# A chunked RWKV-7 recurrence inside one fused block: 64-column products turned into whole-array products, and the output products gathered behind the loop

## The chip, the cores and the metric

The kernel runs on one core of one Trainium2 chip. The metric is the device time of one execution in microseconds (us). Below, PE is the tensor engine (matmuls), PEld its weight loads, DVE the vector engine, ACT the scalar engine, POOL the GpSimd engine, SP the engine that issues most DMAs.

## The reference, cut to what matters

One transformer block on 512 tokens of width 2048: an RWKV-7 time mix with 16 heads of 64, a sparse attention, gates, an output projection and an MLP. The change touches the time mix alone. For each head it scans over the tokens:

```python
def step(S, inp):
    r_t, w_t, k_t, v_t, kk_t, a_t = inp
    sa = jnp.einsum('bhij,bhj->bhi', S, -kk_t)
    S = S * w_t[:, :, None, :] + sa[..., None] * (kk_t * a_t)[:, :, None, :] + v_t[..., None] * k_t[:, :, None, :]
    return S, jnp.einsum('bhij,bhj->bhi', S, r_t)
```

S is a 64x64 state per head. All arrays are float32.

## The kernel before, in words

The scan is done in chunks of 64 tokens: eight chunks (`NCH`), and heads in pairs, so eight passes (`hp`, 0 to 7) over a pair of heads. `stage1` does for each pair: `gates` (the inputs of the scan), `inner` (all products inside a chunk, for all chunks at once) and `outer` (the recurrence from chunk to chunk). The change is in `outer`, L536 to L575.

The state M of both heads is one 128x128 tile: head 0 in rows and columns 0 to 63, head 1 in 64 to 127, zeros elsewhere (`self.Ms`, two tiles that take turns). For chunk c, `outer` issues in this order:

- L550, PE: WT of the chunk (128 rows, 64 columns) times M, into half of the partitions of the PSUM tile `pu` (tile name `seq`, one buffer). L551, DVE: VU of the chunk is U0 less that product.
- L552, PE: M times the queries AR of the chunk, added into 64 columns of the PSUM tile `py`, which collects the output of all chunks.
- L556, POOL: the decayed state Mf, for the next M.
- L557, a "pump": some steps of other work for PE (below).
- L562, PE: for each head the keys KBn (64 columns) times VU (64 columns), into 64 partitions of the PSUM tile `pm` (`seq` again). L566 and L568, DVE: the next M, one instruction a head.
- L572, PE: for each head VU (64 columns) times the scores S (64 columns), added into `py`.
- L575, another pump.

So M waits for `pm`, the next L550 for M, VU for L550, and `pm` for VU: a chain that goes back and forth between PE and DVE. A float32 matmul of the program stands in the trace as two records of PE and two weight loads; they are called passes below. A matmul whose output has 64 columns of weights works in a 128x64 part of the array (the trace writes 128*64), and the two heads of L562 and of L572 sit in the two halves.

The other work is a list of projection jobs (`add_job`): each step (`step`, L104 to L106) is three matmuls with 128x128 weights and 512 columns, in the split format that the kernel uses for its projections, and counts as three filler passes. `pump(t)` adds t times a rate to a credit and issues steps while the credit lasts; the rate of a pair of heads is set so that its jobs (`FILL`) last through it. What is left is issued by `drain()` at the end of the pair. PE and POOL run in the order written; the order of DVE, ACT and SP is chosen by the scheduler of the compiler. The weights of a step come by DMA (L66), are rounded by ACT (L67), and DVE forms the remainder (L68). After the loop come a pump (L579), ACT's square and copy of `py` (L581, L583), a pump, and the sums over a head (L599) for the norm.

Of the kernel before, what the change touches and what calls it, by code (L numbers as in the profile page):

```python
# [17 lines left out]
OP = mybir.AluOpType  # L18
# [5 lines left out]
C = 64  # L24
NCH = T // C
# [27 lines left out]
class Kern:  # L53
# [236 lines left out]
    def stage1(self):  # L290
        nc, tc, a = self.nc, self.tc, self.a
        with ExitStack() as ctx:
# [56 lines left out]
            for j in range(2):  # L349
                m = p.tile([128, 128], F32, name=f"M{j}")  # L350
                nc.gpsimd.memset(m, 0.0)
# [40 lines left out]
    def t2(self, name, bufs=1):  # L392
        return self.p1.tile([128, T], F32, name=name, bufs=bufs)
# [142 lines left out]
    def outer(self, hp, cur):  # L536

        nc, p, pp, t2, big = self.nc, self.p1, self.ps1, self.t2, self.big
        AR, KBn, VU, f, bv, g, S, U0, WT = (cur[n] for n in ("AR", "KBn", "VU", "f", "bv", "g", "S", "U0", "WT"))

        py = pp.tile([128, T], F32, name="py", bufs=1)
        M = None
        for c in range(NCH):
            q, cp = c % 2, c // 2
            us = slice(64 * q, 64 * q + 64)
            if M is None:
                nc.scalar.copy(VU[us, c], U0[us, cp])
            else:
                pu = pp.tile([128, T], F32, name="seq", bufs=1)
                nc.tensor.matmul(pu[us, 0:128], WT[:, cp, us], M, start=True, stop=True)  # L550
                nc.vector.scalar_tensor_tensor(VU[us, c], pu[us, 0:128], -1.0, U0[us, cp], op0=OP.mult, op1=OP.add)  # L551
                nc.tensor.matmul(py[:, C * c:C * c + C], M, AR[:, 1, C * c:C * c + C], start=False, stop=False)  # L552
            Mn = self.Ms[c % 2]
            if M is not None and c < NCH - 1:
                Mf = p.tile([128, 128], F32, name="Mf", bufs=1)
                nc.gpsimd.tensor_scalar(Mf, M, f[:, c:c + 1], None, op0=OP.mult)  # L556
            self.pump(PUMP["u"])  # L557
            if c < NCH - 1:
                pm = pp.tile([128, T], F32, name="seq", bufs=1)
                for h in range(2):  # L560
                    hs = slice(64 * h, 64 * h + 64)
                    nc.tensor.matmul(pm[hs, 0:64], KBn[:, c, hs], VU[:, c, hs], start=True, stop=True)  # L562
                for h in range(2):
                    hs = slice(64 * h, 64 * h + 64)
                    if M is None:
                        nc.vector.tensor_scalar(Mn[hs, hs], pm[hs, 0:64], f[hs, c:c + 1], None, op0=OP.mult)  # L566
                    else:
                        nc.vector.scalar_tensor_tensor(Mn[hs, hs], pm[hs, 0:64], f[hs, c:c + 1], Mf[hs, hs],  # L568
                                                       op0=OP.mult, op1=OP.add)
            for h in range(2):  # L570
                hs = slice(64 * h, 64 * h + 64)
                nc.tensor.matmul(py[hs, C * c:C * c + C], VU[:, c, hs], S[:, h, c, 64:128],  # L572
                                 start=c == 0, stop=c == NCH - 1)
            if c < NCH - 1:
                self.pump(PUMP["m"])  # L575
            M = Mn


        self.pump(PUMP["gn0"])  # L579
        sq = t2("sq")  # L580
        nc.scalar.activation(sq, py, AF.Square)  # L581
        y = t2("tha")
        nc.scalar.copy(y, py)  # L583
        self.pump(PUMP["gn2"])
        ye = self.head_rsqrt(self.head_sums(sq), 1.0 / 64, GN_EPS, None)
        self.pump(PUMP["gn3"])
        rs = self.head_bcast(ye)
        nc.vector.tensor_tensor(y, y, rs, OP.mult)
        nc.vector.scalar_tensor_tensor(y, y, self.par("lnx_w", hp), bv, op0=OP.mult, op1=OP.add)
        yo = t2("yo")  # L590
        nc.vector.scalar_tensor_tensor(yo, y, self.par("lnx_b", hp), g, op0=OP.add, op1=OP.mult)
        nc.sync.dma_start(self.yd[hp], yo)
# [957 lines left out]
```

## Time and profile before

| | |
|---|---|
| time, median of 3 runs | 3124.81 us (3119.63 to 3130.18) |
| time of the profiled execution | 3125.73 us |
| its span, first to last instruction | 3124.0 us |
| granted TensorE clock, mean of the span | 0.993 of full speed |
| PE busy | 3050.8 us, 98% of the span |
| PE weight loads busy | 2591.8 us, 83% |
| DVE, ACT, POOL busy | 59%, 38%, 19% |

The profiled execution is one run; its span leaves out 1.7 us before the first and after the last instruction. A pass of PE lasts longer than the distance to the next one, since passes are pipelined: what a pass costs is read from the starts of neighbours, not from its length. Stage 1's eight pairs of heads lie between about 95 and 950 us.

### The profile page before, as it was taken

The page shows a single profiled execution, that of the slowest core. Times are in us where ns is not written, and L with a number is a line of the kernel's source. Part 1 is how long each engine was busy: PE and PEld are TensorE (multiplying, and loading weights), DVE is VectorE, ACT ScalarE, POOL GpSimd, SP SyncE. Part 2 cuts the span into 40 slices and gives each one's busy share as a digit, 9 for nine tenths or more (in the row PEclk, how much of TensorE's full clock was granted, in tenths as well). Part 3 has the DMA queues.
Part 4 walks back from the last instruction along what each step waited for, and adds up shares of the span by engine and source line. Part 5 has one row for each costly group of instructions (what it writes and reads, how often), then busy time and mean ns, then how long its engine had stood idle before and what let it go on. Part 6 is the DMA issues. An engine that isn't in the chain of part 4 may idle for free.

```text
span 3124.0 us, 49657 instructions
## 1 busy us (share of the span) xinstructions
PE 3050.8 (98%) x19296; PEld 2591.8 (83%) x19296; DVE 1855.4 (59%) x3312; ACT 1192.9 (38%) x2031; POOL 588.6 (19%) x613
## 2 busy tenths in 40 slices
PE   9999999999999999999999899999999999999998
PEld 7777777777777877787888899999997888888998
DVE  7855756575563457775464877777775232344565
ACT  4322333233232335654333444444444232232454
POOL 2312222231231000001221533333330000000012
PEclk9999999999999999999999999999999999999999
DMA  4222222222224422225543344444446243253465
GB/s 163 82 85 75 82 78 74 71 82 83 77 79 142 135 95 65 65 78 189 169 144 128 133 135 128 131 135 134 128 130 204 94 139 103 94 165 118 148 193 176
DMA packets 165596, 369.28 MB, mean 118 GB/s; under 512 B 18672, under 2 KB 24304, under 8 KB 157168
## 3 DMA queue, kind: packets, MB, share of 16 engines
q1 hardware_dynamic: 154080, 339.28, 33.7%
q10 hardware_dynamic: 10640, 24.73, 2.1%
q8 instruction: 151, 2.47, 0.3%
q0 software_dynamic: 640, 2.10, 0.2%
q14 instruction: 85, 0.70, 0.1%
HBM read 322.06 MB, written 41.94 MB: 117 GB/s over the span
## 4 chain that ended last, share of the span: by engine, by line
PE 62%; DVE 2%; DMA 1%; POOL 1%; issue 0%; ACT 0%; SPq 0%; DVEq 0%; ACTq 0%; POOLq 0%
PE acc L1263 20%; PE acc L104 13%; PE acc L106 12%; PE acc L105 12%; PE po L1043 1%; PE sc L1010 1%; PE pt L1032 1%; DMA wraw<-w_down 1%; DVE wlo L68 0%; DMA u<-ud 0%; PE sc L954 0%; POOL rb L1177 0%; DMA raw<-w_up 0%; PE po L989 0%; POOL sq L1175 0%
## 5 line engine op out<-in xcount | busy, mean ns | idle before, releaser
L67 ACT CAST whi<-wraw 128x512 fp32r<-128x512 f32 x752 | 465.8, 620 | 1065.9 <-PE acc L105 989.2
L68 DVE TENSOR_TENSOR wlo<-wraw,whi 128x512 fp32r<-128x512 f32 x752 | 530.7, 707 | 567.6 <-ACT whi L67 560.0
L104 PE MATMUL acc<-xn,whi 128*128 128x512 f32 x1472 | 611.5, 415 | 1.3 <-DVE th L387 1.3
L106 PE MATMUL acc<-xn,wlo 128*128 128x512 f32 x1472 | 578.2, 393 | 0.0
L105 PE MATMUL acc<-xn,whi 128*128 128x512 f32 x1472 | 577.1, 392 | 0.0
L104 PE MATMUL acc<-xs,whi 128*128 128x512 f32 (+1 forms) x1280 | 449.5, 351 | 5.4 <-ACT xs L932 5.4
L105 PE MATMUL acc<-xs,whi 128*128 128x512 f32 (+1 forms) x1280 | 449.1, 351 | 2.0 <-DVE xs L933 2.0
L106 PE MATMUL acc<-xs,wlo 128*128 128x512 f32 (+1 forms) x1280 | 448.8, 351 | 0.1
L1263 PE MATMUL acc<-hx,hs 128*128 128x256 f32 x2048 | 369.8, 283 | 3.1 <-ACT hs L1248 3.1
L106 PEld LDWEIGHTS acc<-xn,wlo 128*128 128x128 f32 x1472 | 277.3, 188 | 61.6
L104 PEld LDWEIGHTS acc<-xn,whi 128*128 128x128 f32 x1472 | 278.1, 189 | 60.0 <-issue 6.5
L1263 PEld LDWEIGHTS acc<-hx,hs 128*128 128x128 f32 x2048 | 317.4, 190 | 3.3 <-ACT hs L1248 3.3
L105 PEld LDWEIGHTS acc<-xn,whi 128*128 128x128 f32 x1472 | 278.7, 189 | 46.0
L1263 PE MATMUL acc<-hx,ls 128*128 128x256 f32 x1024 | 289.2, 282 | 2.1 <-DVE ls L1249 2.1
L1263 PE MATMUL acc<-hx,h 128*128 128x256 f32 x1536 | 277.8, 283 | 5.0 <-ACT h L1240 5.0
L104 PEld LDWEIGHTS acc<-xs,whi 128*128 128x128 f32 x1280 | 241.4, 189 | 41.2 <-ACT xs L932 6.4
L105 PEld LDWEIGHTS acc<-xs,whi 128*128 128x128 f32 x1280 | 241.4, 189 | 38.4 <-DVE xs L933 3.5
L106 PEld LDWEIGHTS acc<-xs,wlo 128*128 128x128 f32 x1280 | 241.4, 189 | 35.5 <-DVE wlo L68 0.5
L1263 PEld LDWEIGHTS acc<-hx,h 128*128 128x128 f32 x1536 | 237.7, 190 | 5.4 <-ACT h L1240 5.4
L1249 DVE TENSOR_TENSOR ls<-s,hs 128x1024 fp32r<-128x1024 f32 x128 | 184.5, 1441 | 74.6 <-ACT hs L1248 74.5
L1263 PE MATMUL acc<-hx,l 128*128 128x256 f32 x768 | 216.5, 282 | 1.8 <-DVE l L1241 1.8
L1263 PEld LDWEIGHTS acc<-hx,ls 128*128 128x128 f32 x1024 | 195.8, 191 | 2.3 <-DVE ls L1249 2.3
(354 smaller groups left out, 4225.3 us busy)
## 6 DMA issues: line engine op xcount, KB each, us to landing
wraw<-w_down SPq DMA_DIRECT2D x320, 256.0 KB, 3.2
raw<-w_up SPq DMA_DIRECT2D x64, 1024.0 KB, 5.2
wraw<-w_gate SPq DMA_DIRECT2D x128, 256.0 KB, 3.0
wraw<-w_rkv SPq DMA_DIRECT2D x96, 256.0 KB, 3.1
wraw<-w_o SPq DMA_DIRECT2D x64, 256.0 KB, 3.1
ud<-f ACTq DMA_DIRECT2D x32, 512.0 KB, 6.2
u<-ud SPq DMA_DIRECT2D x32, 512.0 KB, 5.3
thd<-th SPq DMA_DIRECT2D x32, 256.0 KB, 3.5
```

Source lines behind the costliest of these rows:

```text
L67: nc.scalar.copy(hi, raw)
L68: lo_eng.tensor_tensor(lo, raw, hi.bitcast(F32), OP.subtract)
L104: nc.tensor.matmul(ps, hi[:, j], xh, start=opens and k == 0, stop=False)
L105: nc.tensor.matmul(ps, hi[:, j], xl, start=False, stop=False)
L106: nc.tensor.matmul(ps, lo[:, j], xh, start=False, stop=close and last)
L1010: nc.tensor.matmul(ps[:, 0:n], q, self.kst[h][:, x, br, 0:n], start=x == 0, stop=x == 1)
L1032: nc.tensor.transpose(pt[:, b], s[:, 128 * b:128 * b + 128], self.ident)
L1043: nc.tensor.matmul(self.o[j][64 * h:64 * h + 64, 128 * i:128 * i + 128], self.vn[:, b, v0:v0 + 64], pT[h][:, b], start=False, stop=i == 3 ...
L1249: nc.vector.tensor_tensor(l, s, h.bitcast(F32), OP.subtract)
L1263: nc.tensor.matmul(o, w[wi][part][:, 128 * i:128 * i + 128], x[:, xi, xp], start=kh == 0 and i == 0 and m == 0 and slot in opens, stop=kh ...
```

## The change

Three edits in `outer`. L550 takes both chunks of WT (128 columns of weights) and writes all 128 partitions of `pu`; the half that is read is the same. The two products of L562 become one with 128 columns of weights and 128 columns of VU; of its result the two diagonal blocks are read. L572's sixteen products leave the loop and are issued behind it, first the eight chunks of head 0, then the eight of head 1; `py` is opened by the product of L552 of chunk 1 in place of L572 of chunk 0. The pumps stay where they are.

```diff
-                nc.tensor.matmul(pu[us, 0:128], WT[:, cp, us], M, start=True, stop=True)
+                nc.tensor.matmul(pu[:, 0:128], WT[:, cp], M, start=True, stop=True)
                 nc.vector.scalar_tensor_tensor(VU[us, c], pu[us, 0:128], -1.0, U0[us, cp], op0=OP.mult, op1=OP.add)
-                nc.tensor.matmul(py[:, C * c:C * c + C], M, AR[:, 1, C * c:C * c + C], start=False, stop=False)
+                nc.tensor.matmul(py[:, C * c:C * c + C], M, AR[:, 1, C * c:C * c + C], start=c == 1, stop=False,
+                                 skip_group_check=True)
...
-                for h in range(2):
-                    hs = slice(64 * h, 64 * h + 64)
-                    nc.tensor.matmul(pm[hs, 0:64], KBn[:, c, hs], VU[:, c, hs], start=True, stop=True)
+
+                nc.tensor.matmul(pm[:, 0:128], KBn[:, c], VU[:, c], start=True, stop=True)
...
-                        nc.vector.tensor_scalar(Mn[hs, hs], pm[hs, 0:64], f[hs, c:c + 1], None, op0=OP.mult)
+                        nc.vector.tensor_scalar(Mn[hs, hs], pm[hs, hs], f[hs, c:c + 1], None, op0=OP.mult)
                     else:
-                        nc.vector.scalar_tensor_tensor(Mn[hs, hs], pm[hs, 0:64], f[hs, c:c + 1], Mf[hs, hs],
+                        nc.vector.scalar_tensor_tensor(Mn[hs, hs], pm[hs, hs], f[hs, c:c + 1], Mf[hs, hs],
                                                        op0=OP.mult, op1=OP.add)
-            for h in range(2):
-                hs = slice(64 * h, 64 * h + 64)
-                nc.tensor.matmul(py[hs, C * c:C * c + C], VU[:, c, hs], S[:, h, c, 64:128],
-                                 start=c == 0, stop=c == NCH - 1)
             if c < NCH - 1:
                 self.pump(PUMP["m"])
             M = Mn
+        for h in range(2):
+            hs = slice(64 * h, 64 * h + 64)
+            for c in range(NCH):
+                nc.tensor.matmul(py[hs, C * c:C * c + C], VU[:, c, hs], S[:, h, c, 64:128], start=False,
+                                 stop=c == NCH - 1, skip_group_check=True)
```

## Rows read from the trace of the kernel before

**Rows 1.** The profile's page: busy time by engine.

```profile
PE 3050.8 (98%) x19296; PEld 2591.8 (83%) x19296; DVE 1855.4 (59%) x3312; ACT 1192.9 (38%) x2031; POOL 588.6 (19%) x613
```

**Rows 2.** Windows: stage 1, and the loop of the first pair; columns in the second line.

```profile
core 0: us, PE busy (x) PEld busy (x) DVE busy (x) ACT busy (x) POOL busy (x), PEclk, DMA share, GB/s
160.00:950.00 790.00, 771.94 (x5129) 590.53 (x5128) 476.81 (x948) 239.74 (x449) 203.13 (x286) 1.00 0.24 79
162.58:190.84 28.26, 28.26 (x166) 19.22 (x165) 12.14 (x30) 5.60 (x9) 3.63 (x6) 1.00 0.22 75
```

**Rows 3.** Timeline of PE, one chunk (start, length to the last end, operation, count).

```profile
168.13 0.39 PE L105 MATMUL acc<-xn,whi 128*128 128x512 f32 x1
168.36 0.39 PE L106 MATMUL acc<-xn,wlo 128*128 128x512 f32 x1
168.68 0.43 PE L550 MATMUL seq<-M,WT 128*64 128x128 f32 x2
169.04 0.43 PE L552 MATMUL py<-AR,M 128*128 128x64 f32 x2
169.28 0.47 PE L104 MATMUL acc<-xn,whi 128*128 128x512 f32 x1
169.60 0.39 PE L105 MATMUL acc<-xn,whi 128*128 128x512 f32 x1
169.82 0.40 PE L106 MATMUL acc<-xn,wlo 128*128 128x512 f32 x1
170.15 0.34 PE L562 MATMUL seq<-VU,KBn 128*64 128x64 f32 x4
170.32 0.29 PE L572 MATMUL py<-S,VU 128*64 128x64 f32 x4
170.53 0.50 PE L104 MATMUL acc<-xn,whi 128*128 128x512 f32 x1
170.87 0.39 PE L105 MATMUL acc<-xn,whi 128*128 128x512 f32 x1
...
172.80 0.43 PE L550 MATMUL seq<-M,WT 128*64 128x128 f32 x2
```

**Rows 4.** Timeline of the weight loads around L741, then around L702, whole-array products.

```profile
265.36 1.09 PEld L741 LDWEIGHTS un<-Z,Q 128*128 128x128 f32 x8
...
260.79 0.97 PEld L702 LDWEIGHTS un<-Df,N 128*128 128x128 f32 x8
261.69 0.19 PEld L104 LDWEIGHTS acc<-xn,whi 128*128 128x128 f32 x1
```

**Rows 5.** Timeline of PE at the same two places.

```profile
265.35 0.39 PE L106 MATMUL acc<-xn,wlo 128*128 128x512 f32 x1
265.58 1.00 PE L741 MATMUL un<-Z,Q 128*128 128x64 f32 x8
...
262.03 0.39 PE L105 MATMUL acc<-xn,whi 128*128 128x512 f32 x1
```

**Rows 6.** Instructions of L550 and L572 (ns min/median/max).

```profile
L550 PE MATMUL seq<-M,WT x112: 272/298/324, 164.6 to 946.7; 128*64 128x128 f32 x112
...
L572 PE MATMUL py<-S,VU x256: 221/222/271, 162.7 to 948.8; 128*64 128x64 f32 x128
```

**Rows 7.** Timeline at the end of the first pair's loop.

```profile
190.52 0.40 PE L106 MATMUL acc<-xn,wlo 128*128 128x512 f32 x1
190.85 0.34 PE L572 MATMUL py<-S,VU 128*64 128x64 f32 x4
191.11 0.50 PE L104 MATMUL acc<-xn,whi 128*128 128x512 f32 x1
191.23 0.60 ACT L581 ACTIVATE sq<-py 128x512 f32<-128x512 f32 x1 [1.09 <-PE py L572]
```

**Rows 8.** Timeline of DVE in the chunk of rows 3.

```profile
168.85 0.69 DVE L68 TENSOR_TENSOR wlo<-wraw,whi 128x512 fp32r<-128x512 f32 x1 [1.79 <-ACT whi L67]
169.57 0.28 DVE L551 SCALAR_TENSOR_TENSOR VU<-seq,U 64x128 f32<-64x128 f32 x1
170.60 0.60 DVE L568 SCALAR_TENSOR_TENSOR M<-seq,f,Mf 64x64 f32<-64x64 f32 x2 [0.75 <-PE seq L562]
```

**Rows 9.** Timeline in the pair with the fewest fillers.

```profile
497.05 0.29 DVE L568 SCALAR_TENSOR_TENSOR M<-seq,f,Mf 64x64 f32<-64x64 f32 x1
497.56 0.19 PEld L550 LDWEIGHTS seq<-M,WT 128*64 128x64 f32 x2 [0.36 <-DVE M L568]
```

**Rows 10.** Waits of PE, 160 to 950 us (us in total, times, longest).

```profile
PE big L619 <- ACT sq L612: 12.1, 8, 3.9
...
PE seq L550 <- DVE M L568: 0.8, 1, 0.8
```

## The prediction

> **What bounds the kernel now.** I read the page first, then windows of the stage that changes, then the timeline of one chunk, last the waits. The page has PE busy 98% of the span and every other engine at 59% or less [rows 1]. In the first pair's loop PE is busy in all of 28.26 us, at a granted clock of 1.00 (the upper level, 2.4 GHz), while DVE fills 12.14 us and DMA moves 75 GB/s [rows 2]. In all of stage 1 PE waits only once in the recurrence, 0.8 us for M; its one large wait is 12.1 us for L612, behind the loop [rows 10]. So a microsecond that PE's order saves in `outer` comes off the end, as long as DVE's two answers per chunk (VU, M) still arrive before PE asks for them.
>
> The timeline shows what a chunk costs. Fillers follow each other at 0.23 us (168.13 to 168.36). From the filler ahead of L550 to the second filler behind L552 it is 168.36 to 169.60, 1.24 us, of which two fillers explain 0.46: the two products cost 0.78. From the filler ahead of L562 to the second behind L572 it is 169.82 to 170.87, 1.05 us, so these cost 0.59 [rows 3]. Together **1.37 us a chunk**. The columns streamed explain little of it: each place where 128*64 meets 128*128 has a gap. L550 starts 0.32 us after a filler, not 0.23, and L552 starts 0.36 us after L550's two passes [rows 3].
>
> **The change, part by part.** *L550 and L562 over the whole array.* The nearest rows are L741 and L702, float32 with 128x128 weights. L741 starts 0.23 us after its filler, the plain pitch [rows 5], because its first weight load starts at 265.36 [rows 4], with that filler's own start [rows 5]: it is loaded while the filler streams. Inside, L702's eight loads take 0.97 us, 0.19 each, so seven distances are 0.78: **0.111 us a pass** [rows 4]. Out again: L104's load starts at 261.69 [rows 4] and the second filler at 262.03 [rows 5]; 0.34 is one load plus one pitch, so leaving costs nothing more. A chunk then has six whole-array passes (two each of L550, L552, and the joined L562): 6 x 0.111 = 0.67 us. L552's passes stream only 64 columns but are bound by their loads, as L741's are; I count them at 0.111 too. Saved: 1.37 - 0.67 = 0.70 us a chunk. The loop has 56 products of L550 (112 passes [rows 6]) and 7 x 8 = 56 of L562; the chunk without L550 and the one without L562 pair up, so 56 x 0.70 = **39.3 us saved**. This includes L572 leaving the loop.
>
> *The group at the end.* The last chunk's L572 already stands alone between fillers: 190.85 to 191.11, 0.26 us for four passes [rows 7]. The four are two steps of a pair: the heads' passes start together in the two halves. In rows 3 the four last 0.29 us to the end of the last; one lasts 0.22 [rows 6]; so all four start within 0.07 us and a step takes about 0.058. The new group has 32 passes, first sixteen of one half, then sixteen of the other; no neighbour shares the step. It needs 32 steps for two: 30 more, x 0.058 = 1.74 us a pair, x 8 = **13.9 us added**. No row has many passes in one half alone, so the step is bounded: below by half of a 128-column pass, 0.055 (13.2 us); above by a full whole-array pass, 0.111 (26.6 us). I take 0.058, as both halves of rows 3 run at that step side by side, each loading its next weights while it streams.
>
> Against this the Trainium skill ("TensorE: Matmul & The Clock Gate", Part 3, The mechanism) says that a weight load overlaps running matmuls only in another row group, and here all passes use all rows; by it load and stream would add and the group would be the upper bound. The loads of rows 4 and 5, which start with the filler's stream over the same rows, disagree.
>
> A second rule of the Trainium skill ("TensorEngine Tiling (Array Packing)", When to Use Tiling) recommends half-array tiles for 64-column weights, up to twice as fast; by it the joined L562 would lose. The 0.59 us of rows 3 are mostly not streaming, so the trace does not bear that out for a lone pair between fillers.
>
> *What is moved and what waits.* No DMA, ACT or POOL instruction is added or moved. DVE reads the same shapes, the second head from other columns of the same PSUM tile. ACT's square of `py` (0.60 us [rows 7]) waits for the whole group as it waited for the last L572. The pumps behind it still lie between it and the head sums, and cover it; without them it would cost its 0.60 us and the chain to L619 would grow by as much. That chain's 12.1 us [rows 10] starts at the group's end and stays.
>
> *VectorE's answers get less time.* The wait of a product sits at its weight load (L550's load waits for M [rows 9]), so the answer must be there 0.111 us ahead of the product's turn. With one step between, L562's turn comes 4 x 0.111 + 3 x 0.23 = 1.13 us after L550's start, so VU must end by about 1.0. In rows 8 VU ends at 169.85, 1.17 us after L550's start at 168.68, behind an L68 of 0.69 us: some 0.2 us late, with 0.05 for the signal (an estimate, between nothing and the 0.22 from M's end to the load in rows 9). L68 meets VU in few chunks; I count 0.2 us a pair, 1.6 us. In the pair with fewest fillers M ends at 497.34 and L550 is held by it to 497.56 already [rows 9]; that chunk and the one with the 0.8 us wait gain nothing or less: 1.0 us. Bounds: 0, and the third rival. Behind a late L562 stands every later filler, since PE keeps its order.
>
> **The sum**: -39.3 + 13.9 + 1.6 + 1.0 = -22.8 us, from the profiled execution's 3125.7 us (span 3124.0 and 1.7 around it) to 3102.9. The median of the runs shown is 0.9 us lower, so I forecast 3102. About 0.3%, 9.4 us, is what a measurement of this kernel can tell from no change.
>
> **The rivals.**
> 1. *One half alone can't load while it streams.* The group costs 0.111 a pass: -39.3 + 26.6 + 2.6 = -10.1 us, 3115. For it: no row has such a run; against it: L550's second pass starts 0.16 us after the first (0.43 to the end of two, 0.27 for the second [rows 3, 6]), and a 64-column load, a 128-column stream and another load one after the other would need 0.22. Chance 0.08. The rule of the first page above gives this time; the trace speaks against it.
> 2. *The whole-array products are not loaded ahead*, because their load carries a semaphore wait: 112 entries, each with an exposed load of 0.111, give 12.4 back: -10.4 us, 3114. For it: L562's waits sit at the load; against it: L741, which waits for ACT's and PE's results too, starts at the plain pitch. This is also the case in which the change does not do what it says. Chance 0.07.
> 3. *VectorE becomes the bound.* Alone, VU ends about 0.77 us after L550's start: 0.11 to the second pass, 0.27 for it [rows 6], 0.11 until DVE starts (as from L562's end at 170.49 to L568 at 170.60 [rows 3, 8]), 0.28 for VU [rows 8]. With a whole L68 ahead of it, it ends at 1.46, 0.49 too late with the signal. If that came in all 56 chunks: -39.3 + 13.9 + 27.4 = +2.0 us, 3127, no gain; from an average wait of 0.45 us a chunk the change costs time. For it: rows 8 have that L68. Against it: DVE is idle for more than half of the loop [rows 2], and chunks with two steps in between have 0.69 us more. Chance 0.05.
> 4. *The group's passes run one after the other at full length*, 0.22 us each [rows 6], since each adds into columns that the pass before wrote: 8 x (32 x 0.222 - 0.26) = 54.8 added, +18.1 us with the waits, 3143: slower. It passes the time before at about 0.15 us a pass. Against it: rows 3 have two passes of the same columns 0.058 us apart. Chance 0.04.
>
> **How the numbers follow.** My forecast has 0.76. Its own ends are -26.1 us (step 0.055, no late answer: -39.3 + 13.2) and -14.9 (0.08 a pass, twice the waits: -39.3 + 19.2 + 5.2), each with 4 us for the scatter of runs that spread from 3119.6 to 3130.2: 3095 to 3114. That takes in the edge of rivals 1 and 2, and so about 8 in 10. Rivals 1 and 2 lie right beyond 9.4 us, so two thirds of their 0.15 count as faster, with the forecast 0.86; the rest and rival 3 as the same, 0.10; rival 4 as slower, 0.04.
>
> **What would show it.** Right: L550 as 128*128 starts 0.23 us after its filler; from that filler to the second behind L552 it is about 0.90, and 0.69 around the joined L562; the group of 32 passes lasts about 2.0 us; the chunk of rows 3 (four steps) drops from 4.12 us between its L550s to 3.42; PE's waits for VU and M stay under 3 us in all. Wrong: a group of 3.5 us or more (rivals 1, 4), L550 still 0.3 us behind its filler (2), or PE waits for L551 and L568 of tens of microseconds (3). A changed order on DVE outside `outer` would be a cause that I have not priced.

## The result, and the profile after

The changed kernel takes 3102.86 us (median of 4 runs, 3098.36 to 3105.68) against 3123.82 for the kernel before: ratio 0.9928, with a 95% interval of 0.9915 to 0.994. The forecast was 3102, in a range of 3095 to 3114. A second comparison of the same two kernels, made beside later runs, gave 0.9924 (0.991 to 0.9937).

The profiled execution's span is 3100.2 us, 23.8 us less than before. Measured from the first pass of L562 to the last pass of the output products and summed over the eight pairs of heads, the recurrence went from 221.1 to 197.8 us, 23.2 us less; the rest of the span is 2902.9 us before and 2902.4 after, and holds the entry of each pair's first L562, which got 0.09 us shorter (0.7 us in eight pairs). So the time came from `outer`, and nowhere else.

The page's busy times (answers to rows 1) and the window of stage 1 (answers to rows 2):

```profile
PE 3026.8 (98%) x19184; PEld 2607.2 (84%) x19184; DVE 1857.7 (60%) x3312; ACT 1192.8 (38%) x2031; POOL 593.2 (19%) x613
```

```profile
160.00:950.00 790.00, 769.69 (x5109) 624.28 (x5108) 483.90 (x960) 245.05 (x458) 207.24 (x299) 0.99 0.26 83
```

PE still bounds the kernel. It has 112 passes fewer, those of the joined L562, and 24.0 us less of busy time, which is the whole gain; its loads are busy 15 us longer, since 128 columns of weights (0.188 us a load) are loaded in place of 64 (0.134). The granted clock is 1.00, the upper level, in each of the eight loops of both kernels, so the clock explains nothing of what the recurrence gained; the 0.99 of this window (1.00 before) comes from stretches outside the loops. The timeline of PE over a chunk, which answers to rows 3:

```profile
164.44 0.40 PE L106 MATMUL acc<-xn,wlo 128*128 128x512 f32 x1
164.67 0.38 PE L562 MATMUL seq<-VU,KBn 128*128 128x128 f32 x2
164.81 0.48 PE L104 MATMUL acc<-xn,whi 128*128 128x512 f32 x1
165.13 0.39 PE L105 MATMUL acc<-xn,whi 128*128 128x512 f32 x1
...
166.74 0.40 PE L106 MATMUL acc<-xn,wlo 128*128 128x512 f32 x1
166.97 0.38 PE L550 MATMUL seq<-M,WT 128*128 128x128 f32 x2
167.19 0.33 PE L552 MATMUL py<-AR,M 128*128 128x64 f32 x2
167.34 0.48 PE L104 MATMUL acc<-xn,whi 128*128 128x512 f32 x1
167.65 0.40 PE L105 MATMUL acc<-xn,whi 128*128 128x512 f32 x1
...
170.70 0.38 PE L550 MATMUL seq<-M,WT 128*128 128x128 f32 x2
```

Both products now start 0.23 us after their filler, the plain pitch. Around L562 it is 164.44 to 165.13, 0.69 us (1.05 before, with L572); around L550 and L552 it is 166.74 to 167.65, 0.91 us (1.24 before). The weight loads of the same place show why:

```profile
166.74 0.42 PEld L550 LDWEIGHTS seq<-M,WT 128*128 128x128 f32 x2
```

L550's first load begins at 166.74 with the start of the filler ahead of it, and so it does in 51 of the 56 chunks. Before, at the chunk of rows 3, it began with the product itself, 0.31 us after its filler (some 0.32 us in 55 of 56), and waited for nothing that the profile shows:

```profile
168.67 0.19 PEld L550 LDWEIGHTS seq<-M,WT 128*64 128x64 f32 x2 [0.35 <-issue]
```

Behind the loop stands the group, which answers to rows 7:

```profile
185.52 0.39 PE L106 MATMUL acc<-xn,wlo 128*128 128x512 f32 x1
185.84 1.90 PE L576 MATMUL py<-S,VU 128*64 128x64 f32 x32
187.67 0.50 PE L104 MATMUL acc<-xn,whi 128*128 128x512 f32 x1
```

It lasts 1.83 us (0.26 before, for the four passes of one chunk), the same to 0.001 us in all eight pairs. The waits of PE in stage 1 (answers to rows 10):

```profile
PE big L620 <- ACT sq L613: 12.4, 9, 3.9
...
PE seq L550 <- DVE M L568: 1.4, 2, 1.2
```

### The profile page after: what moved, and what is told of

Same layout as the page of the kernel before. It is cut to its first block, busy times and chain, and to the rows that moved or that the text cites. A ratio compares the mean times of both kernels' runs of the same rounds, so it can differ in the third digit from the quotient of the medians.

```text
span 3100.2 us, 49489 instructions
## 1 busy us (share of the span) xinstructions
PE 3026.8 (98%) x19184; PEld 2607.2 (84%) x19184; DVE 1857.7 (60%) x3312; ACT 1192.8 (38%) x2031; POOL 593.2 (19%) x613
## 4 chain that ended last, share of the span: by engine, by line
PE 61%; DVE 2%; DMA 1%; POOL 1%; ACT 1%; issue 0%; SPq 0%; DVEq 0%; ACTq 0%; POOLq 0%
PE acc L1264 20%; PE acc L104 13%; PE acc L105 12%; PE acc L106 12%; PE po L1044 1%; PE sc L1011 1%; PE pt L1033 1%; DMA wraw<-w_down 1%; DVE wlo L68 0%; PE sc L955 0%; POOL rb L1178 0%; ACT whi L67 0%; PE po L990 0%; DMA u<-ud 0%; POOL sq L1176 0%
## 5 line engine op out<-in xcount | busy, mean ns | idle before, releaser
L68 DVE TENSOR_TENSOR wlo<-wraw,whi 128x512 fp32r<-128x512 f32 x752 | 531.7, 708 | 571.1 <-ACT whi L67 563.2
L105 PEld LDWEIGHTS acc<-xs,whi 128*128 128x128 f32 x1280 | 241.3, 188 | 38.6 <-DVE xs L934 3.7
```

What stands on the lines that cost most here:

```text
L68: lo_eng.tensor_tensor(lo, raw, hi.bitcast(F32), OP.subtract)
L105: nc.tensor.matmul(ps, hi[:, j], xl, start=False, stop=False)
```

## The experiments

The first four take the change apart, for three theories of where its gain comes from: the meeting places of half-array and whole-array products (A), the passes saved (B), or L572 leaving the loop (C). The others ask what the group's order costs and how near VectorE is to being the bound. Every kernel below is compared with the kernel before by the ratio of their runs; where a loop is quoted, it is the sum over the eight pairs, 221.1 us before and 197.8 in the full change.

**One part alone: L550 over the whole array.**

```diff
-                nc.tensor.matmul(pu[us, 0:128], WT[:, cp, us], M, start=True, stop=True)
+                nc.tensor.matmul(pu[:, 0:128], WT[:, cp], M, start=True, stop=True)
```

> Only L550 over the whole array, the rest as before. Theory A (the cost sits where a half-array product and a whole-array one are neighbours; a whole-array pass costs 0.111 us): from the filler ahead of L550 to the second behind L552 it drops from 1.24 to 0.90 us, 56 x 0.34 = 19 us faster. Theory B (the gain comes from the 112 passes that the joined L562 saves): no change, within 2 us. Theory C (the gain comes from L572 leaving the loop): no change.

Measured: 0.994 (0.9925 to 0.9954), 20 us faster by the medians; the loop is 202.3 us, 18.8 less. The timeline of PE:

```profile
167.79 0.39 PE L106 MATMUL acc<-xn,wlo 128*128 128x512 f32 x1
168.02 0.38 PE L550 MATMUL seq<-M,WT 128*128 128x128 f32 x2
168.24 0.33 PE L552 MATMUL py<-AR,M 128*128 128x64 f32 x2
168.38 0.48 PE L104 MATMUL acc<-xn,whi 128*128 128x512 f32 x1
168.70 0.39 PE L105 MATMUL acc<-xn,whi 128*128 128x512 f32 x1
```

From filler to second filler it is 0.91 us, as in the full change. Theory A holds; B and C expected nothing here. The same number of passes streams the same number of columns, with twice the weights, in 0.33 us less: 56 x 0.33 = 18.5.

**One part alone: L562 joined.**

```diff
-                for h in range(2):
-                    hs = slice(64 * h, 64 * h + 64)
-                    nc.tensor.matmul(pm[hs, 0:64], KBn[:, c, hs], VU[:, c, hs], start=True, stop=True)
+                nc.tensor.matmul(pm[:, 0:128], KBn[:, c], VU[:, c], start=True, stop=True)
```

> Only L562 joined over the whole array; L572 stays behind it in the loop and L550 is as before. Theory A: a new meeting place of the two shapes lies between L562 and L572, so 1.05 us from filler to filler becomes about 1.16: 56 x 0.11 = 6 us slower, with 112 passes fewer. Theory B: 112 x 0.11 = 12 us faster. Theory C: no change.

Measured: 1.0016 (1.0007 to 1.0026), slower; the loop is 227.7 us, 6.6 more. The timeline of PE, in which L560 is the joined product and L570 the old L572:

```profile
164.70 0.39 PE L106 MATMUL acc<-xn,wlo 128*128 128x512 f32 x1
164.94 0.38 PE L560 MATMUL seq<-VU,KBn 128*128 128x128 f32 x2
165.25 0.34 PE L570 MATMUL py<-S,VU 128*64 128x64 f32 x4
165.51 0.50 PE L104 MATMUL acc<-xn,whi 128*128 128x512 f32 x1
165.85 0.39 PE L105 MATMUL acc<-xn,whi 128*128 128x512 f32 x1
```

It takes 1.15 us against 1.05 in rows 3. With 112 passes fewer the kernel is slower: theory B falls. The entry from the filler costs the plain 0.23 us now, but the gap has moved to between L560 and L570.

**One part alone: the group.** L572 goes behind the loop as in the change; L550 and L562 stay in halves, and L552 of chunk 1 opens `py` as in the change.

```diff
-            for h in range(2):
-                hs = slice(64 * h, 64 * h + 64)
-                nc.tensor.matmul(py[hs, C * c:C * c + C], VU[:, c, hs], S[:, h, c, 64:128],
-                                 start=c == 0, stop=c == NCH - 1)
...
+        for h in range(2):
+            hs = slice(64 * h, 64 * h + 64)
+            for c in range(NCH):
+                nc.tensor.matmul(py[hs, C * c:C * c + C], VU[:, c, hs], S[:, h, c, 64:128], start=False,
+                                 stop=c == NCH - 1, skip_group_check=True)
```

> Only L572 moved behind the loop, as in the change; L550 and L562 as before. Theory A: the loop keeps its meeting places and loses two steps of 0.058 a chunk, 56 x 0.116 = 6.5 us, and the group adds 8 x 1.56 = 12.5 us: 6 us slower. Theory B: no change. Theory C: some 23 us faster.

Measured: 1.0018 (1.0008 to 1.0028), slower; the loop is 227.4 us, 6.3 more. Theory C falls. The timeline of PE, in which L563 is the old L562:

```profile
165.53 0.39 PE L106 MATMUL acc<-xn,wlo 128*128 128x512 f32 x1
165.85 0.34 PE L563 MATMUL seq<-VU,KBn 128*64 128x64 f32 x4
166.11 0.50 PE L104 MATMUL acc<-xn,whi 128*128 128x512 f32 x1
166.45 0.40 PE L105 MATMUL acc<-xn,whi 128*128 128x512 f32 x1
```

Without L572 a chunk gets 0.13 us shorter here (0.92 for 1.05), as both meeting places stay; the group of 1.83 us takes more than that back.

**Two parts: L550 and L562 over the whole array, L572 left in the loop.** The diffs of the first two together.

> L550 and L562 over the whole array, L572 left in the loop. Theory A: -19 and +6, 13 us faster than before, 10 us behind the full change, which it shows to be the worth of moving L572 once L562 is whole. Theory B: 12 us faster. Theory C: no change.

Measured: 0.9958 (0.9943 to 0.9973), 14 us faster by the medians; the loop is 210.0 us, 11.0 less. A holds within 2 us; theory B's 12 us would fit this run too, but it fell with L562 joined alone. Beside the full change's 197.8 the group is worth 12 us, once L562 is whole; alone it cost 6.3. Likewise joining L562 cost 6.6 us alone. The two edits pay only together, because only together do they take the half-array neighbours out of the loop. L550 alone gives 18.8 of the full change's 23.2 us; the other two add 4.4 between them, and more only with another order of the group (below).

**The full change once more, and its group in another order.** The second kernel lets neighbouring passes lie in different halves.

```diff
-        for h in range(2):
-            hs = slice(64 * h, 64 * h + 64)
-            for c in range(NCH):
+        for c in range(NCH):
+            for h in range(2):
+                hs = slice(64 * h, 64 * h + 64)
```

> The full change once more, beside the next two on the same chip: 21 to 24 us faster than before.

> The full change with the group in another order: for each chunk head 0, then head 1, so that neighbouring passes lie in different halves. Theory A1 (passes in different halves start side by side, one in the same half follows 0.058 us later): 16 steps for about 29, the group drops from 1.83 to about 1.1 us, 8 x 0.75 = 6 us faster than the full change. Rival A2 (a group's passes go one by one at 0.058 us whatever their half): the group stays at 1.8 to 2.0 us, no change.

Measured: 0.9924 for the full change, and 0.9894 (0.9881 to 0.9908) with alternating heads, 3091.25 us: faster than both kernels. The timeline of PE in the latter:

```profile
185.70 0.39 PE L106 MATMUL acc<-xn,wlo 128*128 128x512 f32 x1
186.01 1.15 PE L576 MATMUL py<-S,VU 128*64 128x64 f32 x32
187.10 0.50 PE L104 MATMUL acc<-xn,whi 128*128 128x512 f32 x1
```

The group lasts 1.08 us in place of 1.83; the loop is 191.9 us, 5.9 less than the full change's 197.8 in the same set. A1 holds. The medians differ by some 10 us and the spans by 8.8, of which the loop explains 5.9. The rest of the span, which is the same code in all these kernels, lies between 2898.5 and 2903.3 us in the runs above, and it goes with the granted clock: leaving out the last 15 us of each span, the three runs with 2898.5 to 2899.0 us (L562 joined, two parts, alternating heads) have 24 to 27 us at the lower level (1.2 GHz), the five with 2901.9 to 2903.3 us have 31 to 34. Between the two kernels compared here it is 27.3 against 30.7 us, which at half the speed makes about 1.7 of the 3 us (an estimate from these figures); what is left is open.

**Fillers moved from one side of the chain to the other**, on top of the alternating heads.

```diff
-... u=0.93, m=1.63,
+... u=1.3, m=1.26,
```

> The run with alternating heads, with part of the filler moved from behind L562 to ahead of it (pump u 1.3 for 0.93, m 1.26 for 1.63). By the timeline of the full change VU is late in 7 chunks, 1.1 us in all, and a chunk with a single step ahead of L550 waits 0.39 us for M. Theory D1 (only the nearest filler covers an answer of VectorE): the waits for VU go, and about 12 chunks with a single step ahead of L550 in place of 1 wait 0.39 us each, so some 3.5 us slower than the run with alternating heads. Rival D2 (VectorE has time to spare on both sides): no change, waits for M within 2.5 us.

Measured: 0.9939 (0.9926 to 0.9951), 14 us slower than with alternating heads; I had expected 3.5. The loop is 197.6 us, 5.7 more, with three filler passes fewer in the last pair: 6.4 us of waiting. The waits of PE in stage 1, then the timeline of PE and DVE at a chunk with one step ahead of L550 (all in this kernel):

```profile
PE un L678 <- DVE D L690: 6.2, 10, 0.9
PE seq L550 <- DVE M L568: 2.7, 4, 1.9
PE un L703 <- ACT Df L697: 1.3, 3, 0.7
```

```profile
488.09 0.40 PE L106 MATMUL acc<-xn,wlo 128*128 128x512 f32 x1
488.20 0.29 DVE L568 SCALAR_TENSOR_TENSOR M<-seq,f,Mf 64x64 f32<-64x64 f32 x1
...
488.64 0.46 PE L550 MATMUL seq<-M,WT 128*128 128x128 f32 x2 [0.15 <-DVE M L568]
```

L550 stands 0.55 us behind its filler, for M, which ends at 488.49. Fourteen chunks have one step there (about 12 were expected). Against a plain stretch twelve of them lose 0.37 to 0.43 us, which is D1's price, and one loses 0.68. The last, in the pair with the fewest fillers, waits 2.1 us, because DVE does work of its own between the two halves of M. Right behind that wait the granted clock (third column from the end) is 0.50, the lower level:

```profile
499.10:502.50 3.40, 3.40 (x13) 2.82 (x12) 0.53 (x3) 0.00 (x0) 0.70 (x1) 0.50 0.23 77
```

Fillers follow each other at 0.43 us there in place of 0.23. No other loop of any kernel here has a stretch at that level; at half the speed it costs about 1.7 of the 6.4 us (an estimate). One case doesn't show whether the wait brought it on. Without it 4.7 us of waiting are left, against the 3.5 expected: D2 falls, and D1 holds in direction and in its price per chunk. By pairs, the loop is 4.0 us longer in the one with the fewest fillers, which has five of the fourteen chunks and the slow stretch; elsewhere the waits for VU that are gone pay for part of it, and five pairs lose about 0.2 us each. Outside the loop PE waits more too (L678, L703: 2.9 us in all with alternating heads, 7.5 here): the pump's rate is shared, and the edit shifted fillers there as well. So this run can't price the loop's side alone.

**The group in blocks.** Four, then two chunks of one head at a time.

```diff
-        for h in range(2):
-            hs = slice(64 * h, 64 * h + 64)
-            for c in range(NCH):
+        for c0 in range(0, NCH, 4):
+            for h in range(2):
+                hs = slice(64 * h, 64 * h + 64)
+                for c in range(c0, c0 + 4):
```

> The full change with the group in blocks: four chunks (eight passes) of head 0, four of head 1, and again. In the full change three passes of head 1 started beside the last three of head 0, which made the group 1.83 us and not about 2.0. Theory A3 (PE takes a pass of the free half early, but from only about three passes ahead): each of three borders hides about three passes, so the group lasts about 0.107 + 0.15 + (31 - 9) x 0.058 = 1.5 us, 2.5 us faster than the full change. Rival A4 (the overlap comes once, when the second half is used for the first time): 1.83 us as in the full change.

> The same with blocks of two chunks (four passes a head). Theory A3: seven borders hide about three passes each, but a block has only four: 31 - 16 to 31 - 14 steps are left, the group lasts 1.1 to 1.3 us, 4 to 6 us faster than the full change and near the alternating order (1.1 us). Rival A4: 1.83 us.

Measured: 0.991 (0.9893 to 0.9928) and 0.9906 (0.9888 to 0.9923). The groups, of four chunks, then of two:

```profile
185.59 1.54 PE L577 MATMUL py<-S,VU 128*64 128x64 f32 x32
187.06 0.50 PE L104 MATMUL acc<-xn,whi 128*128 128x512 f32 x1
```

```profile
186.36 1.20 PE L577 MATMUL py<-S,VU 128*64 128x64 f32 x32
187.49 0.50 PE L104 MATMUL acc<-xn,whi 128*128 128x512 f32 x1
```

They last 1.47 and 1.13 us, where A3 gave 1.5 and 1.1 to 1.3, and A4 1.83. The loops are 195.0 and 192.2 us, 2.8 and 5.6 less than the full change's 197.8 (A3: 2.5, and 4 to 6). In the blocks of four chunks the records that begin a block are to be known by their length (0.270 us, the others 0.222); they start 0.287, 0.575 and 0.862 us into the group. By the series of starts 0.058 us apart each stands 0.17 us, about three passes, ahead of the start of the last pass of the other half's block.

## Why the prediction was right, point by point

**The bound.** In all eight loops PE waits 1.4 us (0.8 before), and the gain in its busy time, 24.0 us, is the gain in the span. That step held.

**0.70 us a chunk.** Measured: 0.91 and 0.69 us between the fillers, less 0.46 each, is 0.68 for the recurrence in place of 1.37; 56 x 0.69 = 38.6 us saved, 39.3 forecast. (One reading in the prediction is loose: the 0.36 us between L550 and L552 run from the first of L550's two passes; from the second it is 0.20.) The 0.111 us a pass from L741 and L702 carried over to L550, L552 and L562. The first kernel of the experiments shows that the gap at the meeting of the two shapes is what went, since nothing but the shape of L550 changed in it.

**The group.** 1.74 us a pair was forecast, 13.9 in all; 1.83 - 0.26 = 1.57 was measured, 12.5. The step of 0.058 us in one half was right; the count of 30 further steps was too high by three, since head 1's first passes ran beside head 0's last. Rivals 1 and 4, at 0.111 and 0.22 us a pass, fall with it. What the Trainium skill ("TensorE: Matmul & The Clock Gate", Part 3, The mechanism) says of loads in one place, that they overlap running matmuls in another row group only (in another it also lets them go ahead into a background weight buffer), the runs contradict: L550's first load, over all rows, starts with its filler at 166.74 us, and passes of one half, over all rows, follow each other at 0.058 us, while each load row lasts 0.138; the measurement decides.

**Late answers.** 2.6 us more of waiting were forecast. Comparing each stretch of fillers and its product with the plain ones, VU is late in 7 chunks, 1.1 us in all (1.6 forecast), and M in 4, 2.05 us, of which 0.85 stood in the kernel before: 1.2 more (1.0 forecast). That is 2.3 us more, and 3.2 in all, just over the 3 us that the prediction named as a sign of being right. The timelines of DVE and PE at the worst VU:

```profile
167.23 0.69 DVE L68 TENSOR_TENSOR wlo<-wraw,whi 128x512 fp32r<-128x512 f32 x1 [1.49 <-ACT whi L67]
167.96 0.28 DVE L551 SCALAR_TENSOR_TENSOR VU<-seq,U 64x128 f32<-64x128 f32 x1
```

```profile
167.88 0.40 PE L106 MATMUL acc<-xn,wlo 128*128 128x512 f32 x1
168.29 0.49 PE L562 MATMUL seq<-VU,KBn 128*128 128x128 f32 x2
```

It is the chunk of rows 8: L68 is ahead of VU, and L562 starts 0.41 us after its filler. So this chunk, from L550 to L550, takes 3.73 us (166.97 to 170.70) and not 3.42: the prediction's figure left out the 0.2 us of lateness that it had itself worked out for this chunk. In all seven chunks L68 is ahead of VU. That is rival 3's mechanism, in 7 of 56 chunks and at 0.14 to 0.28 us in place of 0.49.

All but 0.05 us of the waits for M are in the pair with the fewest fillers. At the longest, 1.46 us, DVE does some 1.5 us of work of its own between the two heads' halves of M:

```profile
494.85 0.27 DVE L568 SCALAR_TENSOR_TENSOR M<-seq,f,Mf 64x64 f32<-64x64 f32 x1
495.05 0.74 DVE L287 TENSOR_TENSOR s_v<-zt 128x256 f32<-128x256 f32 x2
495.71 0.87 DVE L288 SCALAR_TENSOR_TENSOR s_v<-s_v,prm,zt 128x256 f32<-128x256 f32 x2
496.61 0.29 DVE L568 SCALAR_TENSOR_TENSOR M<-seq,f,Mf 64x64 f32<-64x64 f32 x1
```

**The sum.** -38.6 + 12.5 + 2.3 = -23.8; the loop lost 23.2 and the span 23.8 us. -22.8 was forecast: the group was put 1.4 us too high, the saving 0.7 and the waits 0.3, so that the errors cancel in part. That the forecast of 3102 came within 1 us of the median is in part luck; that each term is within 1.4 us is not. Rival 2 falls by the load that starts with its filler.

**The tiling rule.** The Trainium skill ("TensorEngine Tiling (Array Packing)", When to Use Tiling) recommends half-array tiles for 64 columns. Measured it depends on the neighbours: L550 in halves, between whole-array fillers, costs 0.33 us more, while the group, 32 passes together and in alternating halves, runs two passes in 0.058 us, against 0.111 us for one whole-array pass.

## What to carry to other kernels

Read what a small product costs from the starts of its neighbours: here about half of 1.37 us was gaps where half-array and whole-array products meet, and a product with twice the weights was cheaper because it had the shape of the work around it. Such an edit can cost time alone and pay together with another, so count the meeting places that remain, not the passes. What has to stay in halves is best collected once the rest has the other shape (alone it cost 6.3 us), with neighbours in different halves.

## What the runs showed of the hardware that I had not expected

PE starts a pass of the free half early. In the full change head 1's first three passes start 0.754, 0.861 and 0.919 us into the group, and head 0's last at 0.924, although all of head 0's stand ahead in the program. So that PE runs in the order written does not hold for the starts of passes in different halves. (The records do not name a pass's half; it is read from the starts, two series 0.058 us apart side by side, and from the longer first record of a block.) By the blocks this reaches about three passes ahead, at every border; so alternating in blocks of two chunks (1.13 us) is nearly as good as passes that alternate one by one (1.08).
